# One array tile shape in each attention's bursts of small matmuls: 128x32 in the linear attention, 64x64 in the neighbourhood attention

## The chip, the core and the metric

The kernel runs on one core of one Trainium2 chip. The time is device time in microseconds from one execution of the whole program; several executions are taken and the median counts. A separate execution is recorded by the hardware profiler, with the start and length of each instruction on TensorE (PE, and PEld for its weight loads), VectorE (DVE), ScalarE (ACT), GpSimd (POOL) and SyncE (SP).

## What is computed

Two layers of an encoder trunk over 272 positions (256 grid tokens and 16 learned meta tokens) of width 2048, all in float32. Cut to what matters here:

```python
proj = einsum('bld,dp->blp', h, w_in)
gq, gk, gv, gr, glr, nq, nk, nv = split(proj)
y_gla = _gla_mixer(gq, gk, gv, gr, glr, ...)
y_na = _na_mixer(nq, nk, nv, rel_bias)
mix = einsum('blm,md->bld', concatenate([y_gla, y_na]), w_out)
h = layer_norm(ALPHA * h + mix)
h = layer_norm(ALPHA * h + square(relu(h @ w_ff1)) @ w_ff2)
```

`_gla_mixer` is a bidirectional linear attention with 4 heads (keys of 128, values of 256): every position is weighed with every other by a product of decays along the way, forward and backward. `_na_mixer` has 16 heads of width 64: each token of a 4 x 64 grid attends to a window of 4 x 16 around it and to the 16 meta tokens, with a bias by relative place; meta tokens attend to meta tokens. Meta tokens are dropped from the output, so the last layer needs no results for them.

## The kernel before

**Projections.** Nearly all work is weight times activations. A weight block of 128x1024 comes in by DMA (`raw`), ACT rounds it to the fast format (`wh`, line 217), DVE takes the rest (`wl`, line 218), and PE multiplies with both halves (line 252 in `eight`, 264 in `sixteen`, 303 in `by_k`, 313 in `dense`). `raw`, `wh` and `wl` have three buffers each. These matmuls use the whole 128x128 array, 272 columns at a time, or 512 and 256 in the last layer where the low part goes to a second half of the bank.

**Attention between them.** The attention is a set of generators. After each block of projections `pump` advances one foreground and some background generators, so that their instructions come between the projections. A scheduler places each engine's instructions in one fixed order, near the program's own; an engine runs its queue in that order. Each yield of `True` asks for a place of its own for the next burst of PE work. The matmuls of the attention are true float32; each leaves two passes in the trace.

**Array tiles.** A matmul whose stationary operand is smaller than 128x128 uses a tile of the array, given by the rows and columns it takes (the profile prints `128*32`, rows times columns). Its place follows from the partitions of the operands and of the output.

**Linear attention, `gla_head`.** The positions are merged in levels 0 to 8; each level scores neighbouring blocks. The first burst (`group(0, ...)`) does levels 0 to 3, the second (`group(4, rest)` and what follows) levels 4 to 8 and the meta keys. In `group` (lines 627 and 631) every matmul is 128x32 and four of them fill the four column tiles of a bank. After `group(4)` come, on the whole array: level 8, two matmuls of 128 columns (line 678) into bank `ps`; the 16 meta keys against the queries, two of 128 columns (line 682), of whose output only 16 partitions are used; and in layer 0 (`full`) the queries of the meta tokens, two of 16 columns (line 686) into bank `rest`. ACT copies level 8 to `A` (line 683) and the meta scores to `Am` (line 688), DVE the 16-column results (line 687). `rest` also holds the level-4 scores of the meta queries, which DVE reads in line 645. There are 4 heads in each of 2 layers, 8 second bursts in all.

**Neighbourhood attention, `na_pair` and `na_out`.** Two heads are worked on at once, 8 pairs in each layer. The 256 queries stand as two halves of the grid (`t`), with 176 keys each (`NKEY`). `na_pair` computes the scores: for each half and head a matmul of 64 rows (the head width) and 128 columns (the queries), streaming the 176 keys (line 766); in layer 0 also one of 48 columns for each head's meta queries (line 770). Softmax runs on DVE and ACT, then PE transposes values and probabilities in a burst of its own. `na_out(c)` multiplies probabilities and values and is called at the start of the next pair's `na_pair` (`self.due`), so that it forms one burst with that pair's scores; for pair 7 it is called alone. Its line 827 does the 64 rest keys first (`v2`, `p2`, a 64x64 tile), then the 128 own keys (`v1`, `p1`, 128x64), adding both in the bank `po[t]` of the grid half; line 832 does the meta queries in layer 0 (128x64, 16 columns). The result is read out of each bank by `split`: ACT rounds it into the high part, DVE subtracts for the low part (lines 338 and 339), once for each half and once for the meta columns.

Of the kernel before, what the change touches and what calls it, by code (L numbers as in the profile page):

```python
# [7 lines left out]
F32 = mybir.dt.float32  # L8
# [3 lines left out]
ALU = mybir.AluOpType  # L12
PSUM = bass.MemoryType.PSUM

P = 128
D = 2048
DC = D // P
T = 256
NM = 16
L = T + NM  # L20
DEPTH = 2
ROWS, GW = 4, 64
GH, GDK, GDV = 4, 128, 256
NAH, NAD = 16, 64
# [4 lines left out]
NK2 = 48  # L29
NKEY = P + NK2  # L30
# [28 lines left out]
class Trunk:  # L59
# [518 lines left out]
    def gla_head(self, h):  # L578
        nc, n, full, g2 = self.nc, self.n, self.full, self.g2
        qk, dec = self.qk[h], self.decay[h]  # L580
        A = g2.tile([P, 6, P], F32, name="A", tag="A", bufs=1)
        Am = g2.tile([NM, L], F32, name="Am", tag="Am", bufs=1)
        near = g2.tile([P, 2, 2, 32], F32, name="near", tag="near", bufs=1)
        S = g2.tile([P, 2, 2, L], F32, name="S", tag="S", bufs=1)
        U = g2.tile([P, 4, 2, L], F32, name="U", tag="U", bufs=1)
        X = g2.tile([P, 2, P], F32, name="X", tag="X", bufs=1)
# [87 lines left out]
        rest = self.bank() if full else None  # L674
        group(4, rest)
        ps = self.bank()
        for b in range(2):
            nc.tensor.matmul(ps[:, b * P:b * P + P], lhsT=S[:, 0, b, b * P:b * P + P],  # L678
                             rhs=S[:, 1, 1 - b, P - b * P:T - b * P], start=True, stop=True)
        meta = S.rearrange("p j s c -> p (j s c)")[:, T:T + P]  # L680
        for b, q in enumerate((S[:, 1, 1, :P], X[:, 1])):
            nc.tensor.matmul(ps[:, T + b * P:T + b * P + P], lhsT=meta, rhs=q, start=True, stop=True)
        nc.scalar.copy(A[:, 1:4:2, :], ps[:, :T].rearrange("p (s c) -> p s c", s=2))
        if full:
            for b, k in enumerate((S[:, 0, 1, :P], X[:, 0])):
                nc.tensor.matmul(rest[:, T + b * NM:T + b * NM + NM], lhsT=k, rhs=S[:, 1, 0, T:L], start=True, stop=True)
            nc.vector.tensor_copy(A[:, 2:6:3, :NM], rest[:, T:T + 2 * NM].rearrange("p (s c) -> p s c", s=2))
        nc.scalar.copy(Am[:, :T], ps[:NM, T:])
        yield
        am = g2.tile([80, L], F32R, name="am", tag="am", bufs=1)[:, :n]  # L690
        nc.gpsimd.memset(am.bitcast(F32), 0.0)
# [12 lines left out]
        for e in range(2):  # L704
            o = self.bank()[:, :n]
# [5 lines left out]
            c = slice(h * GDV + e * P, h * GDV + e * P + P)  # L711
# [9 lines left out]
        for e in range(2):  # L721
            c = 2 * h + e
            hi, lo = (t[:, :n] for t in self.y[c])
# [29 lines left out]
    def na_pair(self, c, q, k, v):  # L753
        nc, b = self.nc, self.a2
        heads = [slice(hh * NAD, hh * NAD + NAD) for hh in range(2)]
        two = lambda a: a.rearrange("p (t c) -> p t c", t=2)
        bias = b.tile([P, 4, NKEY], F32, name="nb", tag="nb")
        nc.sync.dma_start(bias, self.i["nab"][self.l, c])
        s = b.tile([P, 4, NKEY], F32, name="ns", tag="ns")
        st = b.tile([P, 12], F32, name="nst", tag="nst")  # L760
        if self.due:
            self.due()
        ps = self.spare(2)
        for t in range(2):
            for hh, hs in enumerate(heads):
                nc.tensor.matmul(ps[hh][:, t * NKEY:t * NKEY + NKEY], lhsT=q[hs, NM + t * P:NM + t * P + P], rhs=k[hs, t, :],  # L766
                                 start=True, stop=True)
        if self.full:
            for hh, hs in enumerate(heads):
                nc.tensor.matmul(ps[hh][:, 2 * NKEY:2 * NKEY + NK2], lhsT=q[hs, :P], rhs=k[hs, 0, P:],  # L770
                                 start=True, stop=True)
            meta = self.nms[c % 2]
            sm = meta[:NM, :, :NK2]
        for hh in range(2):
            nc.vector.tensor_tensor(s[:, 2 * hh:2 * hh + 2, :], two(ps[hh][:, :2 * NKEY]), bias[:, 2 * hh:2 * hh + 2, :], ALU.add)
            if self.full:
                nc.vector.tensor_tensor(sm[:, hh, :], ps[hh][:NM, 2 * NKEY:2 * NKEY + NK2], self.qmask, ALU.add)
        pr = self.npr[c % 2]
        self.softmax(s, st, 4, ((s[:, :, :P], s[:, :, :P]), (pr[:, :, :NK2], s[:, :, P:])))
        yield  # L780
        if self.full:
            mt = b.tile([NM, 6], F32, name="mst", tag="mst")
            self.softmax(sm, mt, 2, ((sm, sm),))
        yield
        yield True
        pv, *pts = self.bank(), *self.spare(2)
        for t in range(2):
            nc.tensor.transpose(pv[:, t * P:t * P + P], v[0][:, t, :], self.ident)
        nc.tensor.transpose(pv[:, T:T + P], v[1].rearrange("p t c -> p (t c)"), self.ident)
        for hh, pt in enumerate(pts):  # L790
            for t in range(2):
                nc.tensor.transpose(pt[:, t * P:t * P + P], s[:, 2 * hh + t, :P], self.ident)  # L792
            nc.tensor.transpose(pt[:, T:T + P], pr[:, 2 * hh:2 * hh + 2, :].rearrange("p u c -> p (u c)"), self.ident)
            if self.full and hh:
                nc.tensor.transpose(pt[:, T + P:], meta.rearrange("p u c -> p (u c)"), self.ident)
        v1 = b.tile([P, 2, P], F32, name="v1", tag="v1")
        v2 = b.tile([P, P], F32, name="v2", tag="v2")
        nc.scalar.copy(v1, two(pv[:, :T]))
        nc.vector.tensor_copy(v2, pv[:, T:T + P])
        p1 = b.tile([P, 4, P], F32, name="p1", tag="p1", bufs=1)  # L800
        p2 = b.tile([P, 2, P], F32, name="p2", tag="p2", bufs=1)
        for hh, pt in enumerate(pts):
            nc.scalar.copy(p1[:, 2 * hh:2 * hh + 2, :], two(pt[:, :T]))
            nc.vector.tensor_copy(p2[:, hh, :], pt[:, T:T + P])
        pm = None
        if self.full:
            pm = self.npm[c % 2]
            for hh, hs in enumerate(heads):
                nc.vector.tensor_copy(pm[hs, hh, :], pts[1][hs, T + P:T + P + NM])
        self.due = lambda: self.na_out(c, v1, v2, p1, p2, pm)  # L810
        yield True
        if c == 7:
            self.due()
            yield

    def na_out(self, c, v1, v2, p1, p2, pm):

        nc, self.due = self.nc, None
        heads = [slice(hh * NAD, hh * NAD + NAD) for hh in range(2)]
        po = [self.bank() for _ in range(2)]
        for rest in (True, False):
            for t, ts in enumerate(heads):
                for hh, hs in enumerate(heads):
                    nc.tensor.matmul(po[t][hs, :P], lhsT=v2[ts, hs] if rest else v1[:, t, hs],  # L827
                                     rhs=p2[ts, hh, :] if rest else p1[:, 2 * hh + t, :],
                                     start=rest, stop=not rest)
        if self.full:  # L830
            for hh, hs in enumerate(heads):
                nc.tensor.matmul(po[0][hs, P:P + NM], lhsT=v2[:, hs], rhs=pm[:, hh, :], start=True, stop=True)
        h, lo = self.y[8 + c]
        for t in range(2):
            half = lambda a: a[:, :T].rearrange("p (r t w) -> p t r w", t=2, r=ROWS)[:, t]
            self.split(po[t][:, :P].rearrange("p (r w) -> p r w", r=ROWS), half(h), half(lo))
        if self.full:
            self.split(po[0][:, P:P + NM], h[:, T:L], lo[:, T:L])
        self.done.add(8 + c)


# [412 lines left out]
```

## Time and profile before

| | |
|---|---|
| median of 3 runs | 2330.06 us (2329.34 to 2331.24) |
| profiled execution | 2329.64 us, of which 2327.8 us is the span from the first to the last instruction |
| granted TensorE clock | 0.999 |
| PE matmul busy | 2318.9 us, 18052 passes |
| DVE, ACT, POOL busy | 1522.8, 1222.8, 129.4 us |
| HBM read | 414.03 MB, 179 GB/s over the span |

A row of the timeline reads: start in us, length in us from the first start to the last end, engine, line, operation, output<-inputs, array tile for PE, shape and type of the moving operand, count; in brackets the idle time before it and what ended it. Rows of one line and tile are merged, also where the shape changes within them. A row of the line groups reads: line, engine, operation, output<-input, shapes, count, then busy us and mean ns of one, then idle time before it and what ended that. A row of the waits reads: who waited, for whom, us in total, times, the longest. PE's passes are pipelined: one that follows at once starts before the end that is shown for the one ahead of it, so distances are taken from start to start, and a pass that is longer than others of its form was waiting for its weights.

### The profile page before, as it was taken

The page shows a single profiled execution, that of the slowest core. Times are in us where ns is not written, and L with a number is a line of the kernel's source. Part 1 is how long each engine was busy: PE and PEld are TensorE (multiplying, and loading weights), DVE is VectorE, ACT ScalarE, POOL GpSimd, SP SyncE. Part 2 cuts the span into 40 slices and gives each one's busy share as a digit, 9 for nine tenths or more (in the row PEclk, how much of TensorE's full clock was granted, in tenths as well). Part 3 has the DMA queues.
Part 4 walks back from the last instruction along what each step waited for, and adds up shares of the span by engine and source line. Part 5 has one row for each costly group of instructions (what it writes and reads, how often), then busy time and mean ns, then how long its engine had stood idle before and what let it go on. Part 6 is the DMA issues. An engine that isn't in the chain of part 4 may idle for free.

```text
span 2327.8 us, 44399 instructions
## 1 busy us (share of the span) xinstructions
PE 2318.9 (100%) x18052; PEld 2202.1 (95%) x18052; DVE 1522.8 (65%) x2440; ACT 1222.8 (53%) x2104; POOL 129.4 (6%) x200
## 2 busy tenths in 40 slices
PE   9999999999999999999999999999999999999998
PEld 9999999999999999999999899989988888888888
DVE  5588777775544455547576787778866545666655
ACT  5666665564433344444456666655655334555443
POOL 0021110110000000000020111100100000000000
PEclk9999999999999999999999999999999999999999
DMA  8554545555555566655555555555666565656664
GB/s 265 155 163 155 151 146 169 173 181 181 181 178 179 179 180 182 181 179 176 181 187 165 173 168 156 158 166 186 192 198 191 190 198 190 192 198 213 199 194 150
DMA packets 118300, 419.01 MB, mean 180 GB/s; under 512 B 13512, under 2 KB 14024, under 8 KB 118096
## 3 DMA queue, kind: packets, MB, share of 16 engines
q1 hardware_dynamic: 117808, 415.65, 57.2%
q8 instruction: 141, 2.31, 0.4%
q14 instruction: 63, 0.52, 0.1%
q10 hardware_dynamic: 288, 0.52, 0.1%
HBM read 414.03 MB, written 2.10 MB: 179 GB/s over the span
## 4 chain that ended last, share of the span: by engine, by line
PE 97%; DVE 1%; issue 1%; ACT 0%; DMA 0%; POOL 0%; DVEq 0%; ACTq 0%; SPq 0%; POOLq 0%
PE mm L252 56%; PE mm L264 30%; PE mm L303 4%; PE mm L313 2%; PE bg L303 1%; PE bg L827 1%; PE mm L766 1%; DVE wl L218 0%; PE bg L627 0%; PE bg L468 0%; DVE acc L1057 0%; PE mm L792 0%; PE bg L955 0%; PE mm L516 0%; PE bg L678 0%
## 5 line engine op out<-in xcount | busy, mean ns | idle before, releaser
L218 DVE TENSOR_TENSOR wl<-raw,wh 128x1024 fp32r<-128x1024 f32 (+1 forms) x770 | 938.3, 1225 | 645.1 <-ACT wh L217 546.0
L217 ACT CAST wh<-raw 128x1024 fp32r<-128x1024 f32 (+1 forms) x770 | 805.5, 1047 | 790.5 <-PE mm L252 383.8
L252 PE MATMUL mm<-x,wh 128*128 128x272 f32 (+3 forms) x4544 | 805.7, 294 | 0.0
L252 PEld LDWEIGHTS mm<-x,wh 128*128 128x128 f32 x4544 | 646.8, 188 | 14.9 <-PE mm L766 0.6
L252 PE MATMUL mm<-x,wl 128*128 128x272 f32 (+3 forms) x2432 | 519.7, 284 | 0.0
L252 PEld LDWEIGHTS mm<-x,wl 128*128 128x128 f32 x2432 | 390.8, 188 | 0.0
L252 PE MATMUL mm<-y,wh 128*128 128x272 f32 (+1 forms) x1440 | 235.0, 285 | 0.0
L252 PEld LDWEIGHTS mm<-y,wh 128*128 128x128 f32 x1440 | 199.7, 188 | 0.1
L264 PE MATMUL mm<-x,wh 128*128 128x512 f32 x832 | 193.8, 390 | 0.0
L264 PEld LDWEIGHTS mm<-x,wh 128*128 128x128 f32 x832 | 154.3, 188 | 31.0
L252 PE MATMUL mm<-u,wh 128*128 128x272 f32 (+1 forms) x1056 | 172.1, 285 | 0.0
L264 PE MATMUL mm<-y,wh 128*128 128x512 f32 x688 | 162.3, 389 | 0.0
L264 PEld LDWEIGHTS mm<-y,wh 128*128 128x128 f32 x688 | 128.6, 188 | 26.8 <-issue 0.4
L252 PE MATMUL mm<-y,wl 128*128 128x272 f32 (+1 forms) x720 | 146.5, 285 | 0.0
L252 PEld LDWEIGHTS mm<-u,wh 128*128 128x128 f32 x1056 | 146.3, 188 | 0.0
L264 PE MATMUL mm<-u,wh 128*128 128x512 f32 x496 | 118.3, 391 | 0.0
L252 PEld LDWEIGHTS mm<-y,wl 128*128 128x128 f32 x720 | 112.6, 188 | 0.0
L264 PEld LDWEIGHTS mm<-u,wh 128*128 128x128 f32 x496 | 90.9, 188 | 17.7
L252 PE MATMUL mm<-u,wl 128*128 128x272 f32 (+1 forms) x528 | 107.3, 284 | 0.0
L264 PEld LDWEIGHTS mm<-x,wl 128*128 128x128 f32 x832 | 98.4, 188 | 2.0
L264 PE MATMUL mm<-x,wl 128*128 128x256 f32 x832 | 98.8, 276 | 0.0
L264 PEld LDWEIGHTS mm<-y,wl 128*128 128x128 f32 x688 | 84.3, 188 | 3.0 <-DVE wl L218 0.2
(286 smaller groups left out, 2297.4 us busy)
## 6 DMA issues: line engine op xcount, KB each, us to landing
raw<-in_wff SPq DMA_DIRECT2D x512, 512.0 KB, 3.6
raw<-in_win SPq DMA_DIRECT2D x190, 512.0 KB, 4.0
raw<-in_wout SPq DMA_DIRECT2D x64, 512.0 KB, 3.6
nb<-in_nab SPq DMA_DIRECT2D x16, 352.0 KB, 4.3
xraw<-in_xT SPq DMA_DIRECT2D x7, 272.0 KB, 4.5
out<-out SPq DMA_DIRECT2D x5, 256.0 KB, 3.1
brow<-in_norm SPq DMA_DIRECT2D x4, 256.0 KB, 5.1
gw<-in_wup SPq DMA_DIRECT2D x4, 196.0 KB
```

The costliest lines, as they stand in the source:

```text
L217: self.nc.scalar.copy(h, r)
L218: self.wl = self.nc.vector.tensor_tensor(lo, r, h.bitcast(F32), ALU.subtract).ins
L252: mm(o, lhsT=self.block(w, j), rhs=rhs, start=first and not i, stop=last and i == len(TURNS[once]) - 1)
L264: self.nc.tensor.matmul(o, lhsT=self.block(both[j // 8][low], j % 8), rhs=rhs, start=first and not i + j, stop=bool(last and i and j == 15 ...
L303: self.nc.tensor.matmul(ps[g + m][:, :n], lhsT=self.block(parts[p][0], 4 * j + m if first else 2 * m + j), rhs=acts[k + j][parts[p][1]][:, ...
L313: self.nc.tensor.matmul(o, lhsT=self.block(both[low], i), rhs=rhs, start=not low and k + i % 2 == 0, stop=k == DC - 2 and i % 2 == 1 and n ...
L766: nc.tensor.matmul(ps[hh][:, t * NKEY:t * NKEY + NKEY], lhsT=q[hs, NM + t * P:NM + t * P + P], rhs=k[hs, t, :], start=True, stop=True)
L827: nc.tensor.matmul(po[t][hs, :P], lhsT=v2[ts, hs] if rest else v1[:, t, hs], rhs=p2[ts, hh, :] if rest else p1[:, 2 * hh + t, :], start=re ...
```

## The change

In the linear attention's second burst level 8, the meta keys and the meta queries are cut into 128x32 tiles, as `group` has them. Level 8 becomes eight matmuls of 128 columns. The meta keys (32 of the stationary columns in place of 128) become four matmuls of 64 columns, a quarter of the queries in each column tile, so that the scores lie on four partition groups and ACT copies them with four instructions. The meta queries become eight matmuls of 16 columns and are written ahead of the copy to `A`.

In the neighbourhood attention the scores are cut along the queries into 64x64 tiles, 8 matmuls in place of 4; the meta queries use 64 of the columns in place of 128. In `na_out` the own keys are cut along the keys: the rest keys (turn 0) and the first half of the contraction (turn 1) go to one bank, the other halves (turn 2) to the other, so that each of the banks `po[0]` and `po[1]` holds a part sum for all 256 queries. The meta queries are cut in the same way, four matmuls in place of two. ACT then copies one bank to a new tile `no`, DVE adds the other bank, and `split` reads that tile, both halves of the grid in one go.

```diff
+        rows = [slice(c, c + 32) for c in range(0, P, 32)]
         for b in range(2):
-            nc.tensor.matmul(ps[:, b * P:b * P + P], lhsT=S[:, 0, b, b * P:b * P + P],
-                             rhs=S[:, 1, 1 - b, P - b * P:T - b * P], start=True, stop=True)
-        meta = S.rearrange("p j s c -> p (j s c)")[:, T:T + P]
-        for b, q in enumerate((S[:, 1, 1, :P], X[:, 1])):
-            nc.tensor.matmul(ps[:, T + b * P:T + b * P + P], lhsT=meta, rhs=q, start=True, stop=True)
+            for c in rows:
+                nc.tensor.matmul(ps[c, b * P:b * P + P], lhsT=S[:, 0, b, b * P + c.start:b * P + c.stop],
+                                 rhs=S[:, 1, 1 - b, P - b * P:T - b * P], start=True, stop=True)
+        meta = S.rearrange("p j s c -> p (j s c)")[:, T:T + 32]
+        halves = [q[:, x:x + 64] for q in (S[:, 1, 1, :P], X[:, 1]) for x in (0, 64)]
+        for c, q in zip(rows, halves):
+            nc.tensor.matmul(ps[c, T:T + 64], lhsT=meta, rhs=q, start=True, stop=True)
+        if full:
+            for b, k in enumerate((S[:, 0, 1, :P], X[:, 0])):
+                for c in rows:
+                    nc.tensor.matmul(rest[c, T + b * NM:T + b * NM + NM], lhsT=k[:, c], rhs=S[:, 1, 0, T:L],
+                                     start=True, stop=True)
         nc.scalar.copy(A[:, 1:4:2, :], ps[:, :T].rearrange("p (s c) -> p s c", s=2))
         if full:
-            for b, k in enumerate((S[:, 0, 1, :P], X[:, 0])):
-                nc.tensor.matmul(rest[:, T + b * NM:T + b * NM + NM], lhsT=k, rhs=S[:, 1, 0, T:L], start=True, stop=True)
             nc.vector.tensor_copy(A[:, 2:6:3, :NM], rest[:, T:T + 2 * NM].rearrange("p (s c) -> p s c", s=2))
-        nc.scalar.copy(Am[:, :T], ps[:NM, T:])
+        for i, c in enumerate(rows):
+            nc.scalar.copy(Am[:, 64 * i:64 * i + 64], ps[c.start:c.start + NM, T:T + 64])
...
-                nc.tensor.matmul(ps[hh][:, t * NKEY:t * NKEY + NKEY], lhsT=q[hs, NM + t * P:NM + t * P + P], rhs=k[hs, t, :],
-                                 start=True, stop=True)
+                for part in heads:
+                    at = NM + t * P + part.start
+                    nc.tensor.matmul(ps[hh][part, t * NKEY:t * NKEY + NKEY], lhsT=q[hs, at:at + NAD], rhs=k[hs, t, :],
+                                     start=True, stop=True)
...
-                nc.tensor.matmul(ps[hh][:, 2 * NKEY:2 * NKEY + NK2], lhsT=q[hs, :P], rhs=k[hs, 0, P:],
+                nc.tensor.matmul(ps[hh][:NAD, 2 * NKEY:2 * NKEY + NK2], lhsT=q[hs, :NAD], rhs=k[hs, 0, P:],
...
-        for rest in (True, False):
-            for t, ts in enumerate(heads):
+        for turn in range(3):
+            for i, ks in enumerate(heads):
+                t = i if turn < 2 else 1 - i
                 for hh, hs in enumerate(heads):
-                    nc.tensor.matmul(po[t][hs, :P], lhsT=v2[ts, hs] if rest else v1[:, t, hs],
-                                     rhs=p2[ts, hh, :] if rest else p1[:, 2 * hh + t, :],
-                                     start=rest, stop=not rest)
+                    nc.tensor.matmul(po[i][hs, t * P:t * P + P], lhsT=v1[ks, t, hs] if turn else v2[ks, hs],
+                                     rhs=p1[ks, 2 * hh + t, :] if turn else p2[ks, hh, :],
+                                     start=turn != 1, stop=turn > 0)
+        n = self.n
         if self.full:
-            for hh, hs in enumerate(heads):
-                nc.tensor.matmul(po[0][hs, P:P + NM], lhsT=v2[:, hs], rhs=pm[:, hh, :], start=True, stop=True)
+            for i, hs in enumerate(heads):
+                for o in range(2):
+                    nc.tensor.matmul(po[i][heads[o], T:L], lhsT=v2[hs, heads[o]], rhs=pm[hs, o, :], start=True, stop=True)
         h, lo = self.y[8 + c]
-        for t in range(2):
-            half = lambda a: a[:, :T].rearrange("p (r t w) -> p t r w", t=2, r=ROWS)[:, t]
-            self.split(po[t][:, :P].rearrange("p (r w) -> p r w", r=ROWS), half(h), half(lo))
+        out = self.a2.tile([P, L], F32, name="no", tag="no", bufs=1)[:, :n]
+        nc.scalar.copy(out, po[1][:, :n])
+        nc.vector.tensor_tensor(out, out, po[0][:, :n], ALU.add)
+        grid = lambda a: a[:, :T].rearrange("p (r t w) -> p t r w", t=2, r=ROWS)
+        self.split(out[:, :T].rearrange("p (t r w) -> p t r w", t=2, r=ROWS), grid(h), grid(lo))
         if self.full:
-            self.split(po[0][:, P:P + NM], h[:, T:L], lo[:, T:L])
+            self.split(out[:, T:], h[:, T:L], lo[:, T:L])
```

## The prediction

> **What bounds the kernel now.** I read the page first, then the waits and the busy time of the two stretches that hold the attention, then the timeline of TensorE around single bursts.
>
> ```profile
> span 2327.8 us, 44399 instructions
> PE 2318.9 (100%) x18052; PEld 2202.1 (95%) x18052; DVE 1522.8 (65%) x2440; ACT 1222.8 (53%) x2104; POOL 129.4 (6%) x200
> PE 97%; DVE 1%; issue 1%; ACT 0%; DMA 0%; POOL 0%; DVEq 0%; ACTq 0%; SPq 0%; POOLq 0%
> ```
> ```profile
> 110.00:360.00 250.00, 250.00 (x2643) 244.60 (x2642) 197.58 (x442) 158.93 (x402) 40.43 (x70) 1.00 0.50 153
> 1370.00:1530.00 160.00, 159.88 (x1551) 147.96 (x1550) 121.51 (x251) 106.68 (x277) 23.62 (x44) 1.00 0.51 157
> ```
> ```profile
> DVE wl L218 <- ACT wh L217: 32.8, 38, 2.2
> ACT wh L217 <- PE mm L252: 29.7, 27, 2.1
> PEld bg L686 <- DVE Am L645: 0.2, 1, 0.2
> ```
>
> TensorE (PE) carries 97% of the chain that ended last. In the two attention stretches (columns: length; PE, weight load, DVE, ACT and POOL busy; clock; DMA share; GB/s) it has no idle time worth naming, while DVE works 79% and 76% of them and ACT 64% and 67%. In the waits of 110 to 360 us, ACT's weight conversions stood 27 times behind PE, that is, with all three buffers full: weights are made ahead of use. PE's own wait for another engine's data is one of 0.2 us. So a microsecond taken out of PE's stream there should come off the end. The question is how much the stream shortens.
>
> **A neighbourhood burst in layer 0**, then a row for the size of a slot, the weight loads of the second shape, and the shortest, median and longest pass of two lines:
>
> ```profile
> 209.12 1.04 PE L827 MATMUL bg<-p,v 64*64 64x128 f32 x16
> 209.98 0.24 PE L832 MATMUL bg<-npm,v 128*64 128x16 f32 x4
> 210.16 0.87 PE L766 MATMUL mm<-nk,nq 64*128 64x176 f32 x8
> 210.86 0.32 PE L770 MATMUL mm<-nk,nq 64*128 64x48 f32 x4
> 211.11 0.63 PE L252 MATMUL mm<-x,wh 128*128 128x272 f32 x3
> ```
> ```profile
> 209.14 0.43 PE L827 MATMUL bg<-p,v 64*64 64x128 f32 x5
> ```
> ```profile
> 209.49 0.42 PEld L827 LDWEIGHTS bg<-p,v 128*64 128x64 f32 x8 [0.17 <-issue]
> ```
> ```profile
> L827 PE MATMUL bg<-p,v x256: 269/273/323, 209.1 to 1531.2; 64*64 64x128 f32 x64, 128*64 128x128 f32 x64
> L766 PE MATMUL mm<-nk,nq x128: 309/309/413, 193.1 to 1520.2; 64*128 64x176 f32 x128
> ```
>
> Every fp32 matmul leaves two passes in the records. Passes on different array tiles run together and those on the same tile follow each other; I call the distance a slot. The five 64x64 passes are the last of the first four tiles and all of the second four: 0.43 - 0.27 = 0.16, less the 0.05 that the first four wait for their weights (323 against 269 ns), so a slot of 128 columns is 0.11 us, with four tiles at once. The scores' 176 columns take (210.86 - 210.16 - 0.10) / 4 = 0.15 us a slot, where 0.10 is the first weights' wait (413 - 309). The 16-column pair takes 0.03 and the 48-column pair 0.04 a slot.
>
> The burst has three shapes. The first 64x64 part is done with its second slot at 209.28, the next would start at 209.39; with the new shape's first weights at 209.49 and the wait for them (0.05) it starts at 209.55: this change of shape costs **0.16 us**. The 16-column slots end at 210.04; the scores start in effect at 210.16 + 0.10: **0.22 us**.
>
> *After.* Three turns of two slots (0.66), two of 16 columns (0.06), four of scores (0.60), two of 48 columns (0.09): twice the scores' passes, but on four tiles in place of two, so no more slots. With 0.05 for the first weights the last pass starts at 1.41 us; the change to full tiles stays (last start 210.91 to 211.11, 0.20). So 1.61 us against 211.11 - 209.12 = 1.99: **0.38 us less, seven times**.
>
> ```profile
> 1409.00 1.04 PE L827 MATMUL bg<-p,v 64*64 64x128 f32 x16
> 1410.52 0.32 PE L766 MATMUL mm<-nk,nq 64*128 64x176 f32 x2
> 1410.77 0.50 PE L252 MATMUL mm<-x,wh 128*128 128x512 f32 x1
> ```
>
> In layer 1, without meta queries: 0.05 + 0.66 + three slots of 0.15 to the last start + 0.25 (1410.52 to 1410.77) = 1.41 against 1.77: **0.36 less, seven times**. The first pair of each layer has scores alone: it saves 0.05 of weight wait. The last has the output alone: 0.16. Neighbourhood sum: 7 x 0.38 + 7 x 0.36 + 0.1 + 0.3 = **5.6 us**. What I have not seen is 64x64 with four streams of 176 columns; the nearest row, 64x64 with 128 columns, shows four streams at once, and I take that. The other bound, two tiles of one row group taking turns, is the last rival below.
>
> **The linear attention's second burst.** Head 0 of layer 0, a first burst's end (the 16-column row and what follows it), and a head of layer 1:
>
> ```profile
> 132.46 0.71 PE L627 MATMUL bg<-U 128*32 128x32 f32 x45
> 133.10 0.71 PE L678 MATMUL bg<-S 128*128 128x128 f32 x4
> 134.46 0.74 PE L252 MATMUL mm<-x,wh 128*128 128x272 f32 x4
> ```
> ```profile
> 132.71 0.45 PE L627 MATMUL bg<-U 128*32 128x64 f32 x16
> 120.11 0.21 PE L631 MATMUL bg<-U 128*32 128x16 f32 x2
> 120.26 0.39 PE L252 MATMUL mm<-x,wh 128*128 128x272 f32 x1
> 1476.86 0.23 PE L627 MATMUL bg<-U 128*32 128x64 f32 x2
> 1477.02 0.71 PE L678 MATMUL bg<-S 128*128 128x128 f32 x4
> 1477.93 0.48 PE L252 MATMUL mm<-x,wh 128*128 128x512 f32 x1
> ```
>
> Sixteen 64-column passes on four tiles take 0.45 - 0.22 = 0.23 us, so 0.06 a slot; a 16-column slot is 0.21 - 0.18 = 0.03; leaving 128x32 for full tiles costs 120.11 + 0.03 to 120.26, 0.11, plus 0.10 for the first weights. Before, from the last 128x32 start (132.71 + 0.45 - 0.22 = 132.94) the twelve full-tile passes run at 0.11 each whether they stream 128 columns or 16, and the projections start in effect at 134.54 (the first of them 0.08 late): 1.6 us. After, four slots of 128 columns (0.45), two of 64 (0.12), four of 16 (0.12), then the change of shape that stood ahead of them (0.11 + 0.10): 0.9 us. **0.70 less**. In layer 1 nothing of 16 columns is there: 1476.87 to an effective 1478.02 becomes 0.02 + 0.45 + 0.12 - 0.06 + 0.15 + 0.10 = 0.78: **0.37 less, four times**. 128 columns at 128x32 are not in the trace; the bounds are four streams at once, as with 64 columns, and one after another (0.11 for each of 16 passes, the last rival). I take the nearest row, four at once.
>
> Two heads are different:
>
> ```profile
> 238.14 0.71 PE L678 MATMUL bg<-S 128*128 128x128 f32 x4
> 239.05 0.62 PE L252 MATMUL mm<-x,wh 128*128 128x272 f32 x3
> 239.66 0.30 PEld L686 LDWEIGHTS bg<-S 128*128 128x128 f32 x2 [0.20 <-DVE Am L645]
> 296.39 0.71 PE L678 MATMUL bg<-S 128*128 128x128 f32 x4
> 298.22 0.16 DVE L645 COPY_PREDICATED Am<-mask,bg 16x16 f32<-16x16 uint8 x1
> ```
>
> In heads 2 and 3 of layer 0 the 16-column matmuls stand behind projections and start only when DVE has read the level-4 meta scores out of the same bank (at 239.6 and 298.4). The edit does not touch that wait. If projections stay in between, the burst falls into two and pays one more change of shape each way (0.10 in, the 0.21 out is partly paid): I take 0.50 saved for these, not 0.70. Sum: 2 x 0.70 + 2 x 0.50 + 4 x 0.37 = **3.9 us**.
>
> The Trainium skill, "TensorE: Matmul & The Clock Gate", section "Wait — 56ns, not 53.3ns?", says that starts of matmuls never come closer than about 25 ns, however few columns; the new burst has 40 passes there, so by it four heads would save 0.3 us less and the sum would be near 8.2. The row at 132.46 disagrees: 45 passes start within 0.71 - 0.22 = 0.49 us, 11 ns apart, so I keep the slots.
>
> **What ACT and DVE get.**
>
> ```profile
> L338 ACT CAST y<-bg 128x128 fp32r<-128x128 f32 x32 | 7.0, 269 | 0.7 <-PE bg L827 0.6
> L338 ACT CAST y<-on 128x256 fp32r<-128x256 f32 x8 | 3.2, 406 | 1.1 <-DVE on L724 1.0
> L557 ACT COPY rv<-mm 128x272 f32<-128x272 f32 x8 | 3.0, 380 | 0.0
> L688 ACT COPY Am<-bg 16x256 f32<-16x256 f32 x8 | 2.9, 356 | 0.0
> L647 ACT COPY near<-bg 128x64 f32<-128x64 f32 x8 | 1.6, 197 | 0.1
> L715 DVE TENSOR_TENSOR on<-bg,gate 128x272 f32<-128x272 f32 x8 | 3.1, 432 | 0.0
> ```
>
> Per pair ACT drops two casts (0.54) and gets a copy and a wider cast (0.38 + 0.41): +0.25. DVE's two subtractions are about as long as those casts and give way to an addition (0.43) and a wider subtraction (about 0.41 by the same ratio): +0.30. The meta split stays, reading SBUF now. Per head the one copy of 16x256 becomes four of 64 columns (0.79 - 0.36 = +0.43). Over 16 pairs and 8 heads: ACT +7.4, DVE +4.8 us, in stretches where both idle a fifth to a third. I cost them at nothing; the full weight buffers are the cover. Behind them in their queues stand the weight conversions, for which PE would wait if the cover went. No DMA, SP or POOL instruction moves.
>
> **Sum.** 5.6 + 3.9 = 9.5 us off the profiled execution's 2329.64 (span and 1.84 around it): 2320.1. The median is 0.42 above that execution, so **2320.6 us**.
>
> **Rivals.**
> - *Conversions late.* Every added microsecond on ACT and DVE delays weights: +12.2 in all, 2332.8 if none is hidden, 2326.7 if half is. For: DVE waits for ACT's half 38 times. Against: the 27 times with full buffers. The Trainium skill, "TensorEngine Tiling (Array Packing)", "PSUM Bottleneck", warns that emptying PSUM becomes the limit once tiling speeds TensorE up, and asks for copies taken together; here one copy becomes four.
> - *PE stands for DVE.* If heads 2 and 3 keep the burst whole in the queue, PE reaches the 16-column passes some 0.4 us after the point where the full tiles start now (238.14 and 296.39) and waits for DVE, about 1.05 us in head 2 and 1.6 in head 3. These two then lose 2.65 - 1.4 = 1.25 where I count a gain of 1.0: 2.2 less saved, **2322.8**.
> - *The bursts are not of one shape.* If full-tile work is put inside most of the 24 bursts, as in those two heads, each pays another change in and out, about 0.3: 7 us, **2327.6**.
> - *Tiles take turns* (the slower side). If passes on the column tiles of one row group don't stream at once with this many columns, 16 x 0.11 replaces 4 x 0.11 (+1.3), the 64- and 16-column slots double up likewise (+0.35 each), and every pair's scores take eight slots (+0.6): 4 x 2.0 + 4 x 1.65 + 16 x 0.6 = 24.2, so **2344.8**. It decides once 40% of the overlap is missing. Against it stand the 64-column and 64x64 rows.
>
> **Chances.** Forecast 0.70, PE standing 0.09, late conversions 0.10, split bursts 0.06, turns 0.05. A change of 0.2% (4.7 us) is about what a measurement of this kernel tells from none: faster is below 2325.4, slower above 2334.7. Forecast, standing and under half of the late case are faster: 0.83; the rest of the late case and the splits 0.11; turns and a bad late case 0.06. For the range, unknown gains of a microsecond or two below (2318.5), and above the standing case and half of the late one (2326).
>
> **What would show it.** In the changed profile the pair's burst should be one row group of 64x64 with no issue gap inside, 1.6 us from its first pass to the projections' row (1.4 in layer 1), and the second bursts 0.9 and 0.8 us from the last 64-column pass. New idle time of PE behind the conversions, 0.11 us between any two passes of new tiles, or projections inside bursts would each name its rival. If all bursts shorten as said and the time doesn't follow, the premise that PE sets the end is what is wrong.

## The result and the profile after

The changed kernel takes 2325.42 us in the median (2324.48 to 2327.6, 17 runs), the kernel before 2330.06 in as many runs beside it: a ratio of 0.9982 [0.9976, 0.9988], 4.6 us less. That is less than half of the 9.5 us forecast. The profiled execution has 2325.9 us, with a span of 2324.1.

The page of the changed kernel, its head, the busy times and the shares of the chain of waits:

```profile
span 2324.1 us, 45342 instructions
PE 2311.4 (99%) x18516; PEld 2197.5 (95%) x18516; DVE 1527.8 (66%) x2440; ACT 1230.7 (53%) x2128; POOL 130.1 (6%) x200
PE 96%; DVE 2%; ACT 1%; issue 1%; DMA 0%; POOL 0%; DVEq 0%; ACTq 0%; SPq 0%; POOLq 0%
```

TensorE is busy 7.5 us less than before (2318.9), but its span is only 3.7 us shorter: its idle time has grown from 2327.8 - 2318.9 = 8.9 to 12.7 us. DVE and ACT have 1% more of the chain each. The busy times of the two attention stretches say where (columns as before):

```profile
110.00:360.00 250.00, 247.01 (x2928) 242.92 (x2927) 201.61 (x443) 164.01 (x415) 40.69 (x70) 1.00 0.51 155
1370.00:1530.00 160.00, 159.01 (x1681) 148.02 (x1674) 124.60 (x252) 109.59 (x287) 24.01 (x44) 1.00 0.52 159
```

Before, TensorE stood 0.0 us of the first stretch and 0.1 of the second; now 3.0 and 1.0. The waits of TensorE over the whole span name the engines it stands for:

```profile
PE bg L689 <- DVE Am L645: 2.5, 2, 1.6
PE bg L969 <- ACT sp L338: 1.7, 2, 1.0
PE mm L303 <- DVE nms L786: 0.5, 1, 0.5
PE mm L313 <- DVE nr L539: 0.2, 1, 0.2
```

Line 689 is the meta queries of heads 2 and 3 in layer 0, line 969 the mean behind a head of the linear attention, lines 303 and 313 the projections behind the last pair of a layer: their next banks still hold the pair's scores (line 786) or, for line 313, a part of the values that DVE has yet to copy (line 539). Of these four, the list of before has one of 1.0 us, for the mean.

**The bursts themselves came out as worked out.** A pair of layer 0, then the second burst of head 0, in the timeline of TensorE:

```profile
208.21 0.89 PE L837 MATMUL bg<-p,v 64*64 64x128 f32 x24
208.92 0.25 PE L844 MATMUL bg<-npm,v 64*64 64x16 f32 x8
209.00 0.81 PE L775 MATMUL mm<-nk,nq 64*64 64x176 f32 x16
209.63 0.27 PE L779 MATMUL mm<-nk,nq 64*64 64x48 f32 x4
209.84 0.77 PE L252 MATMUL mm<-x,wh 128*128 128x272 f32 x4
...
132.90 0.69 PE L627 MATMUL bg<-U 128*32 128x32 f32 x44
133.38 0.27 PE L680 MATMUL bg<-S 128*32 128x128 f32 x1
133.39 0.22 PE L627 MATMUL bg<-U 128*32 128x64 f32 x1
133.41 0.63 PE L680 MATMUL bg<-S 128*32 128x128 f32 x15
...
134.02 0.24 PE L689 MATMUL bg<-S,X 128*32 128x16 f32 x6
134.20 0.77 PE L252 MATMUL mm<-x,wh 128*128 128x272 f32 x4
```

The pair takes 209.84 - 208.21 = 1.63 us, 1.61 were forecast. In head 0 the last 64-column pass of `group` starts at 133.39 and the projections in effect at 134.20 + 0.10: 0.91, forecast 0.9. From the first level-8 pass at 133.38 to the last 16-column pass, which starts at 134.02 + 0.24 - 0.18 = 134.08 (0.18 being a lone 16-column pass), are 0.70 us for 40 passes, one every 18 ns.

**Where the time was given back: head 2 of layer 0.** The timeline of the changed kernel, TensorE and DVE rows:

```profile
236.43 0.63 PE L680 MATMUL bg<-S 128*32 128x128 f32 x15
237.00 1.22 DVE L218 TENSOR_TENSOR wl<-raw,wh 128x1024 fp32r<-128x1024 f32 x1
237.10 0.77 PE L252 MATMUL mm<-x,wh 128*128 128x272 f32 x4
238.13 0.28 DVE L808 COPY v<-bg 128x128 f32<-128x128 f32 x1
238.33 0.48 DVE L813 COPY p<-mm 128x128 f32<-128x128 f32 x2
239.24 0.15 DVE L645 COPY_PREDICATED Am<-mask,bg 16x16 f32<-16x16 uint8 x1
239.45 0.26 PE L689 MATMUL bg<-S 128*32 128x16 f32 x8 [1.58 <-DVE Am L645]
```

and one row of the kernel before, the same read:

```profile
239.45 0.15 DVE L645 COPY_PREDICATED Am<-mask,bg 16x16 f32<-16x16 uint8 x1
```

TensorE reaches level 8 1.7 us earlier than before (236.4 against 238.14), the sum of what it had gained so far. DVE's read, which frees the bank for the 16-column matmuls, comes 0.21 us earlier (239.24 against 239.45): ahead of it in DVE's queue stand a weight half and the copies of values and probabilities, one behind the other. So the 16-column matmuls start at 239.45 where they started at 239.66, and nearly all that had been gained by then is gone; TensorE puts four projection passes in between and then stands 1.58 us.

**The mean and the last pair.** The same view at head 3 of layer 1, and at the last pair of layer 0:

```profile
1487.83 0.42 DVE L724 TENSOR_TENSOR grs<-grs,gtn 128x256 f32<-128x256 f32 x1
1488.28 0.40 ACT L338 CAST sp<-grs 128x256 fp32r<-128x256 f32 x1 [1.50 <-DVE grs L724]
1488.74 0.84 PE L969 MATMUL bg<-sp,onesr 128*128 128x256 f32 x2 [0.70 <-ACT sp L338]
...
341.99 0.19 DVE L786 TENSOR_TENSOR nms<-mm,qmask 16x48 f32<-16x48 f32 x1
342.32 0.73 PE L303 MATMUL mm<-y,wh 128*128 128x272 f32 x4 [0.51 <-DVE nms L786]
```

The first follows a chain DVE, ACT, TensorE; in the second the projections' next bank still holds the scores until DVE has read them. Call it the lead by how much a projection pass of the changed kernel starts earlier than the same pass of the kernel before. It grows at every burst and shrinks at five places: at head 2 by about 1.6 us, head 3 of layer 0 by 1.1, the last pair of layer 0 by 0.7, this mean by 1.3, the last pair of layer 1 by 0.5. That is some 5.3 us out of a gross gain of some 9.3. Another 0.4 us is lost ahead of the first changed burst: the projections of this trace already start that much later there (125.26 against 124.82).

What ACT and DVE got, from the line groups:

```profile
L695 ACT COPY Am<-bg 16x64 f32<-16x64 f32 x32 | 6.5, 204 | 0.3
L338 ACT CAST y<-no 128x256 fp32r<-128x256 f32 x16 | 6.5, 407 | 15.8 <-DVE no L848 15.8
L848 DVE TENSOR_TENSOR no<-no,bg 128x272 f32<-128x272 f32 x8 | 3.4, 430 | 0.0
```

The four meta copies cost 204 ns each, against 197 taken from a 64-column copy by the forecast; with the busy times of the page, ACT got 7.9 us more (7.4 forecast) and DVE 5.0 (4.8). The sizes were right. That they cost nothing was not.

### The profile page after: what moved, and what is told of

Same layout as the page of the kernel before. It is cut to its first block, busy times and chain, and to the rows that moved or that the text cites. A ratio compares the mean times of both kernels' runs of the same rounds, so it can differ in the third digit from the quotient of the medians.

```text
span 2324.1 us, 45342 instructions
## 1 busy us (share of the span) xinstructions
PE 2311.4 (99%) x18516; PEld 2197.5 (95%) x18516; DVE 1527.8 (66%) x2440; ACT 1230.7 (53%) x2128; POOL 130.1 (6%) x200
## 4 chain that ended last, share of the span: by engine, by line
PE 96%; DVE 2%; ACT 1%; issue 1%; DMA 0%; POOL 0%; DVEq 0%; ACTq 0%; SPq 0%; POOLq 0%
PE mm L252 56%; PE mm L264 30%; PE mm L303 4%; PE mm L313 2%; PE bg L303 1%; DVE wl L218 1%; PE bg L837 0%; PE bg L627 0%; PE bg L468 0%; PE mm L775 0%; ACT wh L217 0%; DVE acc L1071 0%; PE mm L801 0%; PE bg L969 0%; PE mm L516 0%
```

## The experiments

The theory to be tried: TensorE's stream shortened as forecast, and half of the gain was given back because TensorE now runs ahead of DVE and ACT at a few places. The rival causes were that the added reads slow the weights, that one half of the change does less than thought, and that ACT's instruction order had changed. In the diffs lines are cut to their core. Ratios are to the kernel before, run beside each.

**The two halves alone: e1 and e2.** e1 has the linear attention's edit, e2 the neighbourhood's; the other attention is as before.

> The change in the linear attention alone, the neighbourhood attention as before. My count of its PE time was 3.9 us (0.70 for heads 0 and 1 of layer 0, 0.50 for heads 2 and 3, 0.37 for the four heads of layer 1). Theory A (the added reads on ACT and DVE set the new waits): this part adds 0.43 us of ACT per head and nothing on DVE, so almost all of it should arrive: 3 to 4 us faster, and PE's wait for DVE at the meta queries short. Theory B (the 16-column matmuls wait for DVE's read of the level-4 scores in their bank, at a time that DVE's queue sets whatever PE does): heads 2 and 3 save nothing or lose, 2.0 to 2.9 us faster, PE waiting over 1 us in all at that line.

> The change in the neighbourhood attention alone, the linear attention as before. My count of its PE time was 5.6 us. Theory A: the added copy and addition (0.25 us of ACT and 0.30 us of DVE per pair) stand ahead of the score addition and the weights, so that part comes back as waits: about 3 us faster. Theory B: most of it arrives, 4.5 to 5.5 us, as this part does not touch the bank of the meta queries. If the two parts alone add up to clearly more than the 4.6 us of the whole change, they meet in DVE's queue.

e1: 2327.44 us, 0.9990 [0.9981, 0.9999], 2.6 us below before. That is in the range of theory B, but B's reason is not there: TensorE's wait at the meta queries is 0.2 us, where B expects over 1.

e2: 2329.93 us (2327.42 to 2333.22), 1.0001 [0.9992, 1.0009], outside both ranges. This is the surprise: its bursts are as short as in the full change (in layer 0, from the last projection pass ahead of a pair to the first behind it, 1.84 us in place of 2.21), yet the time is that of before. TensorE's waits in e2:

```profile
PE bg L686 <- DVE Am L645: 2.0, 2, 1.4
...
PE mm L303 <- DVE nms L779: 0.5, 1, 0.5
PE mm L303 <- DVE x L339: 0.4, 1, 0.4
```

The old full-tile meta queries wait for the same read, though the linear attention was not touched. So the wait in heads 2 and 3 is not made by the new tiles of line 689. Nor does it come with a shorter stream as such. The read and the use in head 2, first in e1, then in e2:

```profile
238.50 0.15 DVE L645 COPY_PREDICATED Am<-mask,bg 16x16 f32<-16x16 uint8 x1
238.71 0.26 PE L689 MATMUL bg<-S 128*32 128x16 f32 x8 [0.20 <-DVE Am L645]
...
240.31 0.16 DVE L645 COPY_PREDICATED Am<-mask,bg 16x16 f32<-16x16 uint8 x1
240.52 0.39 PE L686 MATMUL bg<-S 128*128 128x16 f32 x2 [1.38 <-DVE Am L645]
```

In e1 TensorE reaches level 8 1.1 us earlier than in the kernel before (237.03 against 238.14), and DVE's read is 0.95 earlier too (238.50 against 239.45): hardly anything is lost there. In e2 TensorE is 0.5 earlier (237.61) and the read 0.86 later. So DVE's date is not fixed. It moves along with TensorE when the neighbourhood attention is as before, and falls behind with the neighbourhood's edit. In the kernel before, DVE stands for ACT's conversion ahead of the last weight half that it does before this read (e1 has the same pause, 0.93 us):

```profile
237.19 1.23 DVE L218 TENSOR_TENSOR wl<-raw,wh 128x1024 fp32r<-128x1024 f32 x1 [0.95 <-ACT wh L217]
```

In e2, in e3 below and in the whole change this pause is gone, and DVE does three weight halves almost without a break.

In e2's trace the lead falls at the same five places, by 1.4, 0.8, 0.7, 0.7 and 0.5 us: 4.2 of the 5.5 that its bursts save. That trace is of an execution of 2328.66 us, 1.3 below the median. e2's spread is the largest of all runs, and what makes its other executions slower stays open.

**The added reads out: e3.** The matmuls of the change, but ACT copies 16x256 in one instruction and each half is read from its own bank; half of the own keys' contraction and the right columns of the meta scores are left out of what is read.

```diff
-        for i, c in enumerate(rows):
-            nc.scalar.copy(Am[:, 64 * i:64 * i + 64], ps[c.start:c.start + NM, T:T + 64])
+        nc.scalar.copy(Am[:, :T], ps[:NM, :T])
...
-        nc.scalar.copy(out, po[1][:, :n])
-        nc.vector.tensor_tensor(out, out, po[0][:, :n], ALU.add)
...
+            self.split(po[t][:, t * P:t * P + P].rearrange("p (r w) -> p r w", r=ROWS), half(h), half(lo))
```

> The whole change, but its added reads are left out: the neighbourhood result is split straight out of each bank as before, without adding the other bank (so half of the contraction is left out of the result), and the meta scores are copied by one instruction of 16x256 as before (from the level-8 columns, so that these values are not the right ones). PE's stream is that of the changed kernel, ACT and DVE have before's work. Theory A: the lost 5 us come back, 2320.5 to 2321.5. Theory B: the waits stay, within 1 us of the changed kernel, 2324.5 to 2325.5.

2323.78 us, 0.9974 [0.9964, 0.9984]: 1.6 us below the change, between the two ranges, so neither theory alone. The wait in the two heads is shorter, not gone:

```profile
PE bg L689 <- DVE Am L645: 1.5, 2, 1.0
```

**Another bank for the meta queries: e4.** Their results go into `ps`, behind the meta scores, and ACT reads them there; nothing is written any more into the bank that DVE still reads.

```diff
-                    nc.tensor.matmul(rest[c, T + b * NM:T + b * NM + NM], lhsT=k[:, c], ...)
+                    nc.tensor.matmul(ps[c, T + 64 + b * NM:T + 64 + b * NM + NM], lhsT=k[:, c], ...)
...
-            nc.vector.tensor_copy(A[:, 2:6:3, :NM], rest[:, T:T + 2 * NM]...)
+            nc.scalar.copy(A[:, 2:6:3, :NM], ps[:, T + 64:T + 64 + 2 * NM]...)
```

> The whole change, with the 16-column results of the meta queries in free columns of the bank of level 8, read by ACT, so that PE does not wait for DVE's read of the level-4 scores. Theory B: the waits of 1.58 and 0.90 us in heads 2 and 3 of layer 0 go and the two bursts are whole again: 2 to 3 us faster than the changed kernel, 2322.5 to 2323.5. Theory A: PE then waits for the same late DVE and ACT elsewhere, less than 1 us faster than the changed kernel, 2324.5 to 2325.5.

2323.29 us (2322.84 to 2323.69), 0.9972 [0.9961, 0.9982]: 2.1 us below the change, as theory B has it. The row of line 689 is gone from TensorE's waits; part of the lead is lost again further on, at the means (1.7 us before this edit):

```profile
PE bg L969 <- ACT sp L338: 2.2, 3, 1.0
```

**Both: e5.** e3 and e4 together.

> The third and fourth run together: meta queries in the bank of level 8, and the added reads left out (half of the contraction of the neighbourhood attention and the right meta scores are missing from the result, as in the third). The wait for the level-4 scores was worth 2.1 us and the added reads 1.6. If these are two separate costs, 2321.5 to 2322.0, a microsecond from the sum that I predicted. If the added reads cost only by making DVE late for that one read, nothing more than the fourth run, 2323.0 to 2323.5.

2321.26 us (2320.49 to 2321.86), 0.9964 [0.9951, 0.9976]. That is 2.0 below e4 and 0.2 below the range for two separate costs; the two gains add up, and a little more (1.6 and 2.1 alone, 4.2 together, all by medians). The forecast of 2320.6 lies within its scatter, but only with the added reads taken away.

**The old reads by another order: e6.** e4's linear attention; the scores in 64x64; the output with the meta queries first, then the own keys in 128x64, the rest keys in 64x64 last, so that the shape changes less often than before while each half stays in its bank and is read as before.

```diff
+        if self.full:
+            for hh, hs in enumerate(heads):
+                nc.tensor.matmul(po[0][hs, P:P + NM], lhsT=v2[:, hs], rhs=pm[:, hh, :], start=True, stop=True)
-        for rest in (True, False):
+        for rest in (False, True):
```

> A version for use: the linear attention of the fourth run; in the neighbourhood attention the scores in 64x64 tiles, but the output as before, one bank for each half of the grid and nothing added on ACT and DVE, only in another order: meta queries and own keys (128x64) first, rest keys (64x64) last, next to the scores. By the rows this saves one of the two changes of shape in a pair's burst, 0.2 us of PE in place of 0.37, so 16 pairs give up 2.5 us of PE time and win back 1.6 of waits. If PE's time counts in full: 2324. If it is mostly given back in waits for DVE anyway: equal to or below the fourth run, 2322.5 to 2323.3.

2324.02 us, 0.9976 [0.9966, 0.9985], the first of the two cases. From the last projection pass ahead of a pair in layer 0 to the first behind it are 1.99 us where the change has 1.84, so e6 gives up about 0.15 x 14 = 2.1 us of TensorE's gain. It ends only 0.7 us behind e4; that the difference comes from the reads it doesn't add is the likely reason, not a tested one.

**ACT's order: e7.** In the change a weight conversion had slid behind the softmax on ACT ahead of head 2. Here the softmax comes one step later.

```diff
-        self.softmax(s, st, 4, ((s[:, :, :P], s[:, :, :P]), (pr[:, :, :NK2], s[:, :, P:])))
         yield
+        self.softmax(s, st, 4, ((s[:, :, :P], s[:, :, :P]), (pr[:, :, :NK2], s[:, :, P:])))
```

> The changed kernel with one yield moved ahead of the softmax, so that a weight conversion stands ahead of the exponentials on ACT again in the pair before head 2 of layer 0, as it did before the change (in the changed kernel's order it stands behind them, and DVE then has three weight subtractions in a row just ahead of the transposes' copies and the level-4 read). If that exchange made DVE late: PE's wait at the meta queries of head 2 falls from 1.58 us to under 0.8, and the time by about 1 us, 2324.0 to 2324.7. If DVE was at its limit there in any order: the wait stays over 1.2 us and the time within 0.5 us of 2325.4.

2325.35 us, 0.9981 [0.9972, 0.9990]: the time of the change. DVE's read comes at 238.89 and TensorE still stands:

```profile
239.10 0.26 PE L689 MATMUL bg<-S 128*32 128x16 f32 x8 [1.27 <-DVE Am L645]
```

The order on ACT moves DVE's date by a third of a microsecond and is not the main cause.

**The last pair's banks: e8.** e4, and the last pair of each layer takes two banks of the general pool for its scores in place of the two spare ones that the projections need next.

```diff
-        ps = self.spare(2)
+        ps = self.spare(2) if c < 7 else [self.bank() for _ in range(2)]
```

> The fourth run, and the last pair's scores in two of the attention's own banks in place of two of the four banks that the output projection needs next. The changed kernel lost 0.74 and 0.50 us there, PE waiting for DVE to read the scores. If the bank is the reason: 1.0 to 1.3 us below the fourth run, 2322.0 to 2322.3. If PE would wait for DVE's late weights at that place anyway, no difference beyond 0.4 us.

2321.30 us (2320.96 to 2322.5), 0.9965 [0.9952, 0.9977]: 2.0 below e4, more than the 1.0 to 1.3 expected. Beside e4's trace its projections gain 1.1 us at the last pair of layer 0 and 0.7 at that of layer 1, so the gain is at these places, though the waits listed there for e4 (0.5 and 0.2) don't show all of it. This is the fastest kernel that computes everything, 4.1 us below the change and 8.6 below before.

**The means a step later: e9 and e10.** e9 is e8 with one more step between the split of the head's output and its mean's matmuls; e10 has that and e8's line on the kernel before.

```diff
         self.split(src, *parts)
+        if later:
+            yield
         yield True
```

> The eighth run, with the matmuls of the linear attention's mean one pump step later after the sums that they read. In the eighth run PE waits for ACT's cast of these sums three times, 2.2 us in all, the largest wait left in the attention. If that wait is a question of place: 1.5 to 2.2 us faster, 2319.1 to 2319.8. If DVE's lateness then stops PE at another place, or the longer chain of a head holds up the next: 2321 or more.

> The control: the kernel before, its array tiles untouched, with the last pair's scores in the attention's banks (as in the eighth run) and the means a step later (as in the ninth). If these places only cost what the shorter PE stream uncovers, before gains little: 2328.8 to 2330.0. If they are gains in their own right, unconnected with the change: 2327 or less. The difference between this run and the ninth is then what the tiles alone are worth when PE need not wait: I count 9.5 us.

e9: 2326.43 us, 0.9986 [0.9977, 0.9995], in its second case and far into it, 5.1 above e8. e10: 2331.56 us, 1.0008 [0.9999, 1.0016], outside both of its cases. Between the two are 5.1 us, not 9.5. In e9 the wait of the mean is gone, but others stand in its place:

```profile
PE bg L715 <- ACT parts L338: 2.6, 2, 1.3
...
PE bg L837 <- DVE p L813: 0.8, 1, 0.8
```

Together 3.4 us where e8 has 2.2. This trace is of e9's fastest execution (2324.40 us) and so shows only 3.1 of the 5.1: beside e8 its projections are 1.1 us behind between the two attention stretches and 3.0 behind after the second. The later step also puts several bursts in other places of TensorE's queue. What costs the rest was not found.

**e8 without the added reads: e11.**

> The eighth run with the added reads left out (half of the contraction of the neighbourhood attention and the right meta scores are missing from the result). If the added work on ACT and DVE still costs when the two banks no longer make PE wait: 1.0 to 1.6 us faster, 2319.7 to 2320.3. If it cost only through those two banks: within 0.4 us of the eighth run, 2320.9 to 2321.7.

2320.22 us (2319.14 to 2320.45), 0.9958 [0.9944, 0.9971], 1.1 below e8 and without overlap of their times: the first case, the added reads still cost about 1 us when both bank waits are gone (the runs of before beside it are 0.2 us faster than those beside e8). In the traces e11 gains on e8 at two of the means, 0.9 and 0.8 us, and gives 0.4 back at head 3 of layer 0. TensorE's waits of the attention are down to two rows:

```profile
PE bg L966 <- ACT sp L338: 0.9, 1, 0.9
...
PE bg L680 <- DVE y L339: 0.2, 1, 0.2
```

**e8's line alone: e12.** The last pair's banks on the kernel before.

> The kernel before, with one line of the run e8 alone: the scores of the last pair of each layer go to two banks of the general pool in place of the two spare ones. Theory: PE's wait for these banks comes only with the shorter bursts of the change, since in the kernel before TensorE's waits list no such row (after pair 7 the projections of line 303 run on). Then the line is worth nothing here: ratio 0.9995 to 1.0005, and e8's 2.0 us were time that the change had lost there. Rival: the bank is a gain in its own right, whatever the bursts: about 2.0 us less, ratio 0.999. Third: the line moves transposes and output of the last pair to a worse place in the order, as the difference of e10 to the kernel before may hold: 1.0005 to 1.001.

2328.90 us, 0.9996 [0.9987, 1.0005], 0.95 below before: at the edge of the first range, and the interval decides for neither theory. The traces do: beside the kernel before, e12's projections gain 0.4 us at the last pair of layer 0 and 0.5 at that of layer 1, where e8's gain 1.1 and 0.7 on e4's. So by these traces about half of e8's 2.0 us is a gain that the kernel before could have had as well.

## Why the prediction was right in sign and wrong in size

- **The slots and the changes of shape: right.** 1.63 us for a pair against 1.61, 0.91 for head 0 against 0.9, and in layer 1 a pair's burst is 0.35 shorter where 0.36 was said. *Tiles take turns* is excluded by the same rows. The 25 ns between starts that the Trainium skill gives ("TensorE: Matmul & The Clock Gate", section "Wait — 56ns, not 53.3ns?") would make 39 x 25 = 0.98 us of the 0.70 measured for 40 passes; for passes on tiles of the array the trace disagrees.
- **The premise: this failed.** The prediction put it so: "a microsecond taken out of PE's stream there should come off the end". It rested on TensorE's idle time in the stretches being nil. Nil idle time says that the other engines are early enough at today's dates, not by how much. At five places DVE or ACT did not come earlier by as much as TensorE did, and TensorE's idle time rose from 0.1 to 4.0 us in the two stretches. The last sentence of the prediction's last part named this outcome: all bursts shorter, the time not following.
- **Heads 2 and 3: the wrong sign.** "I take 0.50 saved for these" counted only the change of shape. The row of before that was quoted for it, a wait of 0.20 us for DVE's read in head 2, already said that nothing was to spare there: what is saved ahead of that point gets through only if DVE's read moves along. With the linear attention's edit alone it does (e1: 0.95 us earlier, and TensorE stands 0.20); with the neighbourhood's alone it comes 0.86 later (e2); in the whole change TensorE is there 1.7 us earlier and the read only 0.21. e4 takes the wait away and gains 2.1 us. The added reads are part of the lateness (without them, in e3, the read is 0.78 earlier than in the kernel before), ACT's order a third of a microsecond (e7); what makes up the rest of it is not shown. The rival *PE stands for DVE* priced the wait at 2.2 and had a chance of 0.09. That its price came so close is luck: it was tied to the burst staying whole in the queue; in fact projections stay in between and TensorE stands all the same, because its lead is longer than they are.
- **The added reads: "I cost them at nothing" failed, though not as the rival had it.** Their sizes were right (7.9 and 5.0 us). *Conversions late* would have shown at the projections, and in the change the list of TensorE's waits names no weights. What the reads cost, about 1 to 2 us (e11, e5, and e3 with 1.6), is that they stand on ACT and DVE ahead of the reads for which TensorE waits: in e3 DVE's read in head 2 comes at 238.67 in place of 239.24. The Trainium skill warns ("TensorEngine Tiling (Array Packing)", section "PSUM Bottleneck") that copying out of PSUM may become the bottleneck once tiling has made TensorE faster. These 1 to 2 us agree in direction only: TensorE still has 96% of the chain that ended last. The larger part, some 3 to 4 us by e4, e8 and e12, lies in banks that were read too late for a faster TensorE.
- **The last pair: not seen.** Its projections wait for banks that hold scores; the forecast had no term for it. e8 gets 2.0 us from there, of which about one is no loss by the change (e12).
- **The sum again:** with both banks moved (e8) the change gives 8.6 us, with the added reads out as well (e11) 9.5, by the medians and beside runs of before at 2329.9 and 2329.7. The forecast of 9.5 is close to the 9.3 by which the bursts together are shorter in the trace; the change as made leaves 4.6 of it. That e11 comes out at 9.5 as well is in part luck: TensorE still waits 1.1 us in its list, and about one microsecond is what the last pair's banks bring without the tiles as well (e12).

What stays open: why DVE's read falls behind with the neighbourhood's edit even without the added reads, why most executions of e2 are slower than the one that was profiled, and why a later mean costs 5 us in e9.

## What to carry to other kernels

An engine that is busy all the time sets the end only as far as the others keep ahead of it. Before counting a saving on it, look in the trace at each place where it uses a bank or a tile that another engine has to read first, and take the distance from that read's end to its use. Where that distance is nothing, or where there is a wait of 0.2 us already, a saving gets through only if the other engine comes earlier as well, so look at what that engine waits for ahead of its read. Here DVE moved along in e1, where it had kept a pause of 0.9 us, and fell behind where the pause was gone. And when a faster burst gives nothing, move the result to a bank that is free, and test it with one run each, before taking the burst apart. Run the same move on the kernel before, too: here half of one such gain had nothing to do with the change.

## What the runs showed of the hardware

Sixteen 64x64 passes with 176 columns run four at a time (0.15 us a slot, as two at a time at 64x128 did), and 128x32 passes with 128 columns likewise: 16 of them from 133.38 to the first 64-column pass of line 685 at 133.82. Small tiles start as close as 11 ns apart here (44 passes in 0.69 - 0.22 = 0.47 us, in the row at 132.90). The kernel with the neighbourhood's half of the change (e2) is no faster than the one before, with the whole change 4.6 us faster, with the whole change and two moves of banks 8.6. The gains of the halves, 2.6 and 0.1, do not add up to the 4.6.
